# One encoder layer on one core: another order at the stage heads, second-half tokens and gate weights split ahead, half the norms moved

## The chip, the cores and the metric

The kernel runs on one core of one Trainium2 chip. The metric is the device time of one execution in microseconds (us). Before the change three executions took 2854.31, 2856.01 and 2858.43 us; the median is 2856.01.

## What is computed

The reference is one layer of a bidirectional encoder over 2048 tokens of width 1024, in float32:

```
u    = rmsnorm(x)
proj = u @ w_in                       # 1024 -> 2304: qa ka va qb kb vb
o_a  = rmsnorm(windowed attention, 8 heads, 2 key/value heads, window 128, sink, bias)
o_b  = rmsnorm(mixture of 3 dilated attentions, 8 heads, patterns (128,1) (512,4) (2048,16))
h    = x + rmsnorm(concat(o_a, o_b) @ w_o)
h    = h + rmsnorm(relu(rmsnorm(h) @ w_up)**2 @ w_down)      # 1024 -> 4096 -> 1024
h    = h + rmsnorm(sigmoid(h @ w_gate + b) * (p @ w_ple))    # p: 2048 x 256
```

## The kernel before

**Products.** Every float32 matrix is split into a high part, a rounded copy that ScalarE writes, and a low part, the rest, that VectorE subtracts (`split`, L125, and `split_scaled`, L129, which also multiplies by a gain). A product is three matmuls, high x high, high x low and low x high (L133 to L137, and L171 to L173 where the three are issued piece by piece).

**Engines and order.** SP issues the loads and most stores, ScalarE the stores of projections and of `pled`. The head and the last stage are ordered by the framework's scheduler. From attention A to the end of the MLP the order is written by hand: time is counted in ticks, `later(dt, fn)` puts a step dt ticks ahead, `tick()` runs what is due, and each engine executes its instructions in the order in which they were issued. A tile pool with a tag has a number of slots; a new tile waits until the last user of the slot is done. `raws` (tag wraw) has two slots, `sg` (tag sgt) two, `vr` (tag vraw) two.

**Head.** `prep_tile` (L248) loads a tile of 128 tokens, takes its mean square on ScalarE (`rms`, L120 to L123), the power on GpSimd (L117), scales it on GpSimd (L253), transposes it on TensorE (L144) and splits it (L126, L127). Four tiles make a block of 512 tokens. Four chunks of 128 columns of w_in are loaded and split in 8 pieces each (L130 on ScalarE, L131 on VectorE) before the first projection; then each block goes through the four chunks, and one tile of the next block is prepared after each of them.

**Attention A** has four pairs of heads with 16 items each. At item n = 3 of a pair the next pair's q (`a_half`, GpSimd copies of L233) and bias are fetched. The rest of the q and k projections fills TensorE between the items.

**Attention B** has four pairs of heads; for each the patterns p = 2, 0, 1, and for each pattern eight items. In the first items the kernel issues the loads of v and of biases (`load_text`, then GpSimd copies), of `sel`, and of the first four row blocks of W_o (`load_wo`, `load_wo_k`), which are split by ScalarE and VectorE two ticks after their load, one after the other. Products with the first half of W_o are the filler from tick 11 of the stage on, `ple()` (p @ w_ple) from tick 86. `ple` copies each result from PSUM with ScalarE into an `sgt` tile and stores it to `pled` (L912 to L918). After the last item the mixers of the last pair run out, with two pieces of filler a tick (L976).

**Stage C** (32 steps s, L1280) multiplies by the second half of W_o, adds the first, and does residual and norms. Tokens of the first half are transposed and split into the `vt` tiles; those of the second half go as float32 to `vsp` in DRAM (L1080, L1081). W_up's first chunks are loaded at s = 8 and 15 (`up_weights`, L1111).

**MLP.** Two halves of 1024 tokens; half n // 16, 16 rounds each, 28 ticks a round. Round n runs `down` of its own 256 columns of the hidden layer, as seven products of 2x2 blocks (28 pieces of three matmuls, L1205), and beside it `up` of the next round (L1187). VectorE adds the results to eight `acc` tiles (L1214) and GpSimd does the seventh part (L1212); GpSimd makes the sums and differences of blocks (`combo`, L1105), `pair_of` splits them (L1099, L1100). `up` of round 15 of a half (issued in round 14, and in round 30) is followed by `reload` (L1133): for i = 0, 1 the next content of `vt[i]`, the second half's tokens from `vsp` or the gate's weights, is loaded in four parts and split (L1136 ScalarE, L1137 VectorE, 128x1024 each). At the end of the first half `post` (L1215) does, for each of its eight tiles, squares on ScalarE (L1253), sum and power, the scale on VectorE (L1262), the add of h on GpSimd (L1265) and the store to `hd`; it reads and writes the `acc` tiles, which the second half's first products need again (L1208).

**Last stage.** 16 items of h @ w_gate with the weights in `vt`, from about 2650 us on.

Of the kernel before, what the change touches and what calls it, by code (L numbers as in the profile page):

```python
# [12 lines left out]
F32 = mybir.dt.float32  # L13
# [46 lines left out]
def layer(ctx, tc, a, out):  # L60
# [31 lines left out]
    vsp = dram.tile([2, 128, 8, 512], F32, name="vsp")  # L92
    pled = dram.tile([S, D], F32, name="pled")
# [147 lines left out]
    with ExitStack() as st:  # L241
        pst = st.enter_context(tc.tile_pool(name="pst", bufs=3, space=PSUM, reuse_waits="tile"))
        psm = st.enter_context(tc.tile_pool(name="psm", bufs=5, space=PSUM, reuse_waits="tile"))
        with ExitStack() as st1:
# [3 lines left out]
            def prep_tile(tb, j):  # L248
# [3 lines left out]
                r = rms(xt, xn)  # L252
# [179 lines left out]
    with ExitStack() as st:  # L432
# [38 lines left out]
        def a_item(pair, n):  # L471
# [92 lines left out]
        def feed(t):  # L564
            if t == 57:
# [3 lines left out]
                st_b["b"] = {(0, 2): load_b3(0)}  # L569
            next(fill, None)  # L570
# [53 lines left out]


# [4 lines left out]
    with ExitStack() as st:  # L630
# [11 lines left out]
        def load_bias(pair, i):  # L642
# [12 lines left out]
            def part(hh):  # L655
                text, b = load_text(i, 2 * pair + hh), bs[hh]
                later(2, lambda: copies(text, b))
# [14 lines left out]
        def load_sel():  # L672
            def part(hf):
                raw = raws.tile([32, S // 2], F32, name="sraw", tag="wraw")
                sp.dma_start(raw, a["sel"][:, hf * S // 2 : (hf + 1) * S // 2])
                later(2, lambda: act.activation(sel[:, hf * S // 2 : (hf + 1) * S // 2], raw, AF.Copy))
# [4 lines left out]
        def b_item(pair, p, bank, half):  # L681
# [197 lines left out]
        def ple():  # L879
# [26 lines left out]
            for t in range(16):  # L906
                ph_, pl_ = cur
                for hf in range(2):
# [6 lines left out]
                    mx = sg.tile([128, 512], F32, name="sgt", tag="sgt")  # L915
# [59 lines left out]
        pipe.drain()  # L975
        while mixers:  # L976
            advance()
            next(fill2, None)
            next(fill2, None)
# [131 lines left out]
    def up_weights():  # L1111
# [4 lines left out]
        hl = upw[g] = [fus[g % 3].tile([128, 8, 128], F32R, name="up" + n, tag="up" + n) for n in "hl"]  # L1116

        def hi(q):
# [320 lines left out]
```

## Time and profile before

| | |
|---|---|
| profiled execution, own time | 2857.3 us |
| its span | 2855.5 us |
| mean granted TensorE clock | 0.982 |
| TensorE, matmuls | 2732.8 us (96%) |
| VectorE | 1732.7 us (61%) |
| ScalarE | 1275.2 us (45%) |
| GpSimd | 943.1 us (33%) |
| DMA | 280.86 MB, mean 98 GB/s |

The profile is one execution, with times counted from the start of its span. Engines are called PE (TensorE), PEld (its weight loads), DVE (VectorE), ACT (ScalarE), POOL (GpSimd) and SP (the engine that issues most DMAs). The granted clock is a share of 2.4 GHz; 0.50 is the lower of its two levels, 1.2 GHz, and a mean between 0.50 and 1.00 is a mixture. Busy time says how much an engine does in a stretch; what it waited for is in the waits, and there each wait is put down to the instruction that ended it.

### The profile page before, as it was taken

To read this page: it belongs to the slowest core of one execution; us is meant where nothing else is said; L and a number is where in the kernel's file an instruction comes from. 1 tells how busy PE (TensorE), PEld (TensorE's weight loads), DVE (VectorE), ACT (ScalarE), POOL (GpSimd) and SP (SyncE) were. 2 spreads that over 40 slices of the span, in tenths; PEclk is the share of its full clock that TensorE was granted. 3 is DMA by queue.
4 is the path that set the end of the run, shared out by engine and by line. 5 is a ranking of instruction groups with operands and counts; after the bars stand their busy time and mean duration, and the time that the engine had idled before them with its cause. 6 is when DMAs were issued, how large, how long until landed. Compare 5 with 4: busy or idle time off the path is not lost.

```text
span 2855.5 us, 38726 instructions
## 1 busy us (share of the span) xinstructions
PE 2732.8 (96%) x13952; PEld 2140.4 (75%) x13952; DVE 1732.7 (61%) x3394; ACT 1275.2 (45%) x2928; POOL 943.1 (33%) x942
## 2 busy tenths in 40 slices
PE   7999999997999998999999999998999999998998
PEld 5778866665677776777888888886788888886787
DVE  3210234446656663676777777778777777777665
ACT  4321345556565653556344434445444344344322
POOL 2100033331322311435344334436443344344130
PEclk9999999998999999999999999998999999999999
DMA  5232352315424424772111111214211111112453
GB/s 167 80 122 78 100 159 65 108 65 153 128 72 122 96 93 153 256 249 89 45 59 45 45 59 45 67 63 155 93 45 45 59 45 59 45 52 96 159 195 104
DMA packets 230544, 280.86 MB, mean 98 GB/s; under 512 B 18320, under 2 KB 173968, under 8 KB 227952
## 3 DMA queue, kind: packets, MB, share of 16 engines
q1 hardware_dynamic: 203216, 238.21, 27.1%
q10 hardware_dynamic: 27136, 40.18, 3.9%
q8 instruction: 110, 1.80, 0.3%
q14 instruction: 82, 0.67, 0.1%
HBM read 204.62 MB, written 81.07 MB: 100 GB/s over the span
## 4 chain that ended last, share of the span: by engine, by line
PE 50%; DVE 3%; POOL 1%; issue 1%; ACT 0%; DMA 0%; POOLq 0%; DVEq 0%; SPq 0%; ACTq 0%
PE psd L1205 11%; PE psy L1205 9%; PE psu L172 8%; PE psu L173 8%; PE psu L171 8%; PE psm L135 2%; PE psm L136 2%; PE psm L137 2%; DVE acc L1214 1%; DVE vt L1137 1%; PE pst L144 0%; DVE al L1100 0%; POOL h L1265 0%; DVE dnl L1100 0%; DVE acc L1262 0%
## 5 line engine op out<-in xcount | busy, mean ns | idle before, releaser
L1214 DVE TENSOR_TENSOR acc<-acc,psd 128x512 f32<-128x512 f32 x488 | 332.0, 686 | 197.4 <-PE psd L1205 192.4
L172 PE MATMUL psu<-vt,uph 128*128 128x512 f32 x1024 | 408.8, 399 | 0.0
L173 PE MATMUL psu<-vt,upl 128*128 128x512 f32 x1024 | 406.3, 397 | 0.0
L171 PE MATMUL psu<-vt,uph 128*128 128x512 f32 x1024 | 403.6, 394 | 0.0
L1105 POOL TENSOR_TENSOR tmp<-rl 128x512 f32<-128x512 f32 x64 | 84.0, 1312 | 669.8 <-ACT rl L1193 669.8
L1214 DVE TENSOR_TENSOR acc<-acc,psy 128x512 f32<-128x512 f32 x248 | 170.3, 687 | 107.4 <-PE psy L1205 101.2
L172 PEld LDWEIGHTS psu<-vt,uph 128*128 128x128 f32 x1024 | 193.2, 189 | 48.3
L171 PEld LDWEIGHTS psu<-vt,uph 128*128 128x128 f32 x1024 | 193.7, 189 | 45.3
L745 ACT ACTIVATE e<-e,tm 128x256 f32<-128x256 f32 (+1 forms) x384 | 177.3, 463 | 109.1 <-DVE tm L742 106.9
L173 PEld LDWEIGHTS psu<-vt,upl 128*128 128x128 f32 x1024 | 193.0, 188 | 43.9
L1212 POOL TENSOR_TENSOR acc<-acc,dmp 128x512 f32<-128x512 f32 x128 | 194.3, 1529 | 52.1 <-DVE al L1100 31.5
L1205 PE MATMUL psd<-dnh,ah 128*128 128x512 f32 x512 | 202.6, 396 | 3.1 <-DVE acc L1214 3.1
L1192 ACT ACTIVATE rl<-psu 128x512 f32<-128x512 f32 x128 | 76.4, 597 | 288.8 <-PE psu L173 288.8
L1205 PE MATMUL psd<-dnh,al 128*128 128x512 f32 x512 | 203.9, 398 | 0.0
L131 DVE SCALAR_TENSOR_TENSOR wc<-wraw,pre_mix_t,wc 128x128 fp32r<-128x128 f32 x176 | 57.9, 375 | 239.8 <-ACT wc L130 239.8
L1205 PE MATMUL psd<-dnl,ah 128*128 128x512 f32 x512 | 202.2, 395 | 0.0
L171 PE MATMUL psm<-uhi,wc 128*128 128x512 f32 x448 | 182.0, 411 | 3.7 <-ACT uhi L126 3.7
L742 DVE CUSTOM_DVE_ANT_0 e<-ps_s,b 128x256 f32<-128x256 f32 (+1 forms) x384 | 122.8, 376 | 102.4 <-PE ps_s L729 102.4
L172 PE MATMUL psm<-ulo,wc 128*128 128x512 f32 x448 | 178.0, 398 | 0.0
L173 PE MATMUL psm<-uhi,wc 128*128 128x512 f32 x448 | 177.4, 396 | 0.0
L1205 PE MATMUL psy<-dnh,ah 128*128 128x512 f32 x384 | 154.3, 402 | 18.0 <-DVE acc L1214 10.2
L1205 PE MATMUL psy<-dnh,al 128*128 128x512 f32 x384 | 154.4, 402 | 3.8 <-DVE al L1100 3.8
(692 smaller groups left out, 6247.1 us busy)
## 6 DMA issues: line engine op xcount, KB each, us to landing
upraw<-in_w_up_dram SPq DMA_DIRECT2D x64, 512.0 KB, 4.4
dnraw<-in_w_down_dram SPq DMA_DIRECT2D x64, 512.0 KB, 5.0
xt<-in_x_dram SPq DMA_DIRECT2D x32, 512.0 KB, 4.9
h<-hd SPq DMA_DIRECT2D x32, 512.0 KB, 3.9
wraw<-in_w_in_dram SPq DMA_DIRECT2D x26, 512.0 KB, 4.5
qkd<-sgt ACTq DMA_DIRECT2D x52, 256.0 KB, 2.4
mad<-sgt ACTq DMA_DIRECT2D x32, 256.0 KB, 2.3
pled<-sgt ACTq DMA_DIRECT2D x32, 256.0 KB, 2.0
```

Source lines behind the costliest of these rows:

```text
L131: dve.scalar_tensor_tensor(lo, src, g, hi.bitcast(F32), op0=ALU.mult, op1=ALU.subtract)
L135: pe.matmul(ps, lh(k), rh(k), start=k == 0, stop=False)
L171: pe.matmul(ps, lh(k), rh(k), start=k == 0, stop=False)
L172: pe.matmul(ps, lh(k), rl(k), start=False, stop=False)
L173: pe.matmul(ps, ll(k), rh(k), start=False, stop=k == n - 1)
L742: dve.tensor_tensor_reduce(ej, box["ps"][hh][:, 256 * jj : 256 * jj + w], bs[hh] if p == 2 else bs[hh][:, var], scale=1.0, scalar=3.0e38, ...
L745: act.activation(ej, ej, AF.Exp, bias=tm, scale=-1.0, accum_out=box["dn"][p][:, i : i + 1])
L1105: pool.tensor_tensor(t, x, y, op=op)
L1192: act.activation(rl, ps, AF.Relu)
L1205: pe.matmul(ps, l[:, js], r, start=start and m == 0, stop=m == 2, skip_group_check=True)
L1212: pool.tensor_tensor(t, t, d, op=ALU.add)
L1214: dve.tensor_add(t, t, ps)
```

## The change

- Head: odd tiles of block 0 take their squares on VectorE; the first chunk's splits stand half after tile 2 and half after tile 3; the other three chunks are loaded and split inside block 0's loop, each before its own projection; the next block's tiles are prepared as (0, 1), (2), (3), ().
- Attention A: the first pair's prefetch is at item 6 instead of 3.
- Start of B: the two bias texts of pair 0 are loaded at tick 60 of A; the W_o row blocks are loaded at ticks 2, 2, 6, 7 and each is split four ticks after its load; other loads at 10, 12, 18; sel's copies four ticks after their load.
- End of B: from t = 4 on, ple's copies go to eight slots in one tile; the first three mixer loops take three pieces of filler.
- Stage C: a third `up_weights` at s = 28, split six ticks later.
- MLP: `split_job` loads one 128x512 block of the second half's tokens (rounds 1 to 14) or of the gate's weights (rounds 17 to 28), splits it and stores both parts to `spl`; `reload` only loads them. The first half's `acc` tiles are stored to `yd` at the end of round 15, and `post_job` does their norms, one tile a round, in rounds 17 to 24.

```diff
             prep_tile(0, 0)
             prep_tile(0, 1)
-            wk = load_chunk(w1, 512)
+            wk, raw = w1.tile([128, 2, 8, 128], F32R, name="wc", tag="wc"), load_raw(512)
             prep_tile(0, 2)
+            split_chunk(wk, raw, range(4))
             prep_tile(0, 3)
+            split_chunk(wk, raw, range(4, 8))
             first = [(wk, 512)]
-            for c, pl in ((VA0, w1), (0, wcp), (128, wcp)):
-                first.append((load_chunk(pl, c), c))
             for tb in range(4):
-                for n, (w, c) in enumerate(first):
-                    run(proj_chunk(w, c, tb, psm, pst, "pst"))
-                    if tb < 3:
-                        prep_tile(tb + 1, n)
+                for n in range(4):
+                    if tb == 0 and n < 3:
+                        c, pl = ((VA0, w1), (0, wcp), (128, wcp))[n]
+                        first.append((load_chunk(pl, c), c))
+                    run(proj_chunk(*first[n], tb, psm, pst, "pst"))
+                    for j in ((0, 1), (2,), (3,), ())[n]:
+                        if tb < 3:
+                            prep_tile(tb + 1, j)
...
-                if n == 3 and pair < 3:
+                if n == (3 if pair else 6) and pair < 3:
...
+    def load_wo_first(to):
+        def part(k):
+            halves = load_wo_k(*((wcp, "wc", 2) if k < 2 else (wop, f"wo{k}", 1)), k)
+            later(4, lambda: to.append(halves()))
+
+        for k, dt in enumerate((0, 0, 4, 5)):
+            later(dt, lambda k=k: part(k))
...
-                        st_b["b"][0, 0] = load_bias(0, 1)
-                        later(3, load_sel)
-                        later(5, lambda: load_wo(0, st_b["wa"]))
-                        later(6, lambda: st_b["b"].update({(0, 1): load_bias(0, 2)}))
-                        later(6, lambda: st_b["v"].update({(0, 1): load_v(0, 1)}))
+                        st_b["b"][0, 0] = load_bias(0, 1, st_b["text"])
+                        later(2, lambda: load_wo_first(st_b["wa"]))
+                        later(10, lambda: st_b["b"].update({(0, 1): load_bias(0, 2)}))
+                        later(12, lambda: st_b["v"].update({(0, 1): load_v(0, 1)}))
+                        later(18, load_sel)
...
-                    mx = sg.tile([128, 512], F32, name="sgt", tag="sgt")
+                    if 2 * t + hf == 8:
+                        big = bm.tile([128, 8, 512], F32, name="pst", tag="v1")
+                    mx = big[:, (2 * t + hf) % 8] if t >= 4 else sg.tile([128, 512], F32, name="sgt", tag="sgt")
...
     def reload(i, half):
...
+        vt[i] = new_vt(i)
         def load(q):
...
+            for j in range(2):
+                sp.dma_start(vt[i][j][:, 2 * q : 2 * q + 2].bitcast(F32), spl[half][i][:, j, 2 * q : 2 * q + 2])
         for q in range(4):
-            later((1, 2, 6, 9)[q], lambda q=q: load(q))
+            later(1 + q, lambda q=q: load(q))
+
+    def split_job(half, i, k, at):
...
+        for dt, fn in ((0, fetch), (6, high), (7, low), (9, store)):
+            later(at + dt, fn)
+
+    def post_job(t, at):
...
+        for dt, fn in ((0, fetch), (6, lambda: squares(0)), (7, lambda: squares(1)), (8, rstd), (10, lambda: scale(0)),
+                       (11, lambda: scale(1)), (12, lambda: add(0)), (13, lambda: add(1)), (14, keep)):
+            later(at + dt, fn)
...
-        if s in (8, 15):
-            up_weights()
+        if s in (8, 15, 28):
+            up_weights(6 if s == 28 else 3)
...
+            if 1 <= n < 15:
+                for at in ((0, 14) if n < 3 else (0,)):
+                    split_job(0, *jobs[0].pop(0), at)
+            if 17 <= n < 30:
+                if n < 25:
+                    post_job(n - 17, 0)
+                for at in ((16,) if n < 20 else (0, 14) if n >= 25 else (16,)):
+                    if jobs[1]:
+                        split_job(1, *jobs[1].pop(0), at)
             if n == 15:
-                for t in range(4):
-                    later(14 + 3 * t, lambda t=t: post(0, accs, t, vr, sg, later))
+                for t in range(8):
+                    later(20 + (t // 2 if t < 4 else t), lambda t=t, accs=accs: sp.dma_start(yd[128 * t : 128 * t + 128, :], accs[t]))
```

In `split_job` fetch, high, low and store are a load of 256 KB, a ScalarE copy of 128x512, a VectorE subtraction of 128x512 and a store of 512 KB. In `post_job` fetch loads y and h (two loads of 512 KB into the two slots of vraw), squares are two ScalarE operations of 128x512, rstd three GpSimd operations of one column, scale and add two VectorE operations of 128x512 each, and keep a store of 512 KB.

## Rows read from the trace of the kernel before

**Rows 1.** The page: busy time, share and instructions of TensorE.

```profile
PE 2732.8 (96%) x13952; PEld 2140.4 (75%) x13952; DVE 1732.7 (61%) x3394; ACT 1275.2 (45%) x2928; POOL 943.1 (33%) x942
```

**Rows 2.** Stretches: length, busy per engine (instructions), TensorE clock, DMA share, GB/s.

```profile
0.00:30.00 30.00, 13.28 (x49) 10.35 (x50) 17.70 (x47) 21.67 (x54) 10.51 (x18) 1.00 0.83 245
390.00:400.00 10.00, 5.08 (x29) 3.52 (x28) 1.12 (x5) 2.27 (x7) 3.15 (x4) 0.85 0.45 144
630.00:690.00 60.00, 43.72 (x347) 31.69 (x346) 35.81 (x152) 37.53 (x134) 9.45 (x13) 0.78 0.68 188
1080.00:1100.00 20.00, 11.77 (x41) 8.21 (x40) 8.82 (x16) 6.41 (x13) 1.46 (x2) 0.83 0.46 147
1135.00:1145.00 10.00, 5.44 (x17) 4.18 (x18) 0.43 (x1) 2.65 (x5) 0.00 (x0) 0.83 0.58 197
1279.00:1290.00 11.00, 5.69 (x22) 4.17 (x20) 6.58 (x5) 7.58 (x15) 4.72 (x7) 0.84 0.75 267
1840.00:1882.00 42.00, 42.00 (x182) 33.83 (x181) 30.36 (x42) 17.25 (x31) 17.62 (x12) 1.00 0.16 50
1940.00:2020.00 80.00, 62.89 (x232) 48.82 (x231) 65.56 (x72) 38.48 (x83) 52.23 (x33) 0.87 0.43 143
2605.00:2660.00 55.00, 43.35 (x168) 32.71 (x167) 46.00 (x64) 27.69 (x54) 13.20 (x8) 0.91 0.40 143
2645.00:2660.00 15.00, 11.12 (x48) 8.62 (x47) 9.18 (x19) 8.19 (x26) 0.00 (x0) 0.89 0.47 172
```

**Rows 3.** ScalarE groups of 0-40 us, and a wait of 0-30: total, times, longest.

```profile
L130 ACT ACTIVATE wc<-wraw,pre_mix_t 128x128 fp32r<-128x128 f32 x32 | 10.0, 397 | 0.8 <-DMA wraw<-in_w_in_dram 0.7
L122 ACT ACTIVATE xn<-xt 128x1024 f32<-128x1024 f32 x7 | 7.4, 1056 | 4.4 <-DMA xt<-in_x_dram 4.4
...
PE pst L144 <- POOL xn L253: 15.5, 4, 9.3
```

**Rows 4.** Waits of 390-400 us.

```profile
POOL q L233 <- DMA wraw<-qkd: 7.6, 1, 7.6
```

**Rows 5.** Waits of 630-690 us.

```profile
PE ps_s L729 <- DVE tm L742: 9.5, 3, 9.1
...
ACT wo L130 <- DMA wraw<-in_w_o_dram: 8.2, 1, 8.2
```

**Rows 6.** Waits of 1130-1147 us.

```profile
ACT sgt L916 <- DMA pled<-sgt: 6.3, 2, 4.9
```

**Rows 7.** Waits of 1270-1295 us.

```profile
ACT vs L1080 <- DMA vsp<-vs: 5.4, 2, 3.8
```

**Rows 8.** VectorE groups of 1925-2025 us: busy, mean ns, idle before.

```profile
L1262 DVE SCALAR_TENSOR_TENSOR acc<-acc,rstd,gb 128x1024 f32<-128x1024 f32 x8 | 14.2, 1781 | 3.7 <-POOL rstd L117 3.7
...
L1137 DVE TENSOR_TENSOR vt<-vraw,vt 128x1024 fp32r<-128x1024 f32 x5 | 10.1, 2030 | 0.0
```

**Rows 9.** VectorE in order of time, a steady round: start, us, [idle before].

```profile
1850.11 1.78 DVE L1100 TENSOR_TENSOR al<-tmp,ah 128x512 fp32r<-128x512 f32 x1
...
1854.23 0.68 DVE L1100 TENSOR_TENSOR dnl<-tmp,dnh 128x512 fp32r<-128x512 f32 x1
...
1856.42 0.69 DVE L1214 TENSOR_TENSOR acc<-acc,psd 128x512 f32<-128x512 f32 x1 [0.71 <-PE psd L1205]
...
1859.21 0.69 DVE L1214 TENSOR_TENSOR acc<-acc,psy 128x512 f32<-128x512 f32 x1 [0.62 <-PE psy L1205]
...
1861.30 0.69 DVE L1214 TENSOR_TENSOR acc<-acc,psy 128x512 f32<-128x512 f32 x1 [0.34 <-PE psy L1205]
```

**Rows 10.** GpSimd in order of time, the same round.

```profile
1854.27 1.80 POOL L1105 TENSOR_TENSOR tmp<-dnraw 128x512 f32<-128x512 f32 x1
```

**Rows 11.** SP's waits, 1700-1866 us.

```profile
SPq L1160 <- DVE dnl L1100: 78.2, 4, 19.7
```

**Rows 12.** VectorE groups of 2605-2660 us.

```profile
L1137 DVE TENSOR_TENSOR vt<-vraw,vt 128x1024 fp32r<-128x1024 f32 x8 | 11.8, 1489 | 1.0 <-ACT vt L1136 1.0
```

**Rows 13.** The page, DMA issues: count, size, median us from issue to landing.

```profile
h<-hd SPq DMA_DIRECT2D x32, 512.0 KB, 3.9
```

More of the change, by code (lines that the diff above doesn't have):

```diff
@@ L92, in layer @@
     vsp = dram.tile([2, 128, 8, 512], F32, name="vsp")
+    spl = [[dram.tile([128, 2, 8, 512], F32, name=f"spl{n}{i}") for i in range(2)] for n in "vg"]
+    yd = dram.tile([S // 2, D], F32, name="yd")
     pled = dram.tile([S, D], F32, name="pled")
@@ L569, in feed @@
                 st_b["b"] = {(0, 2): load_b3(0)}
+            if t == 60:
+                st_b["text"] = [load_text(1, hh) for hh in range(2)]
             next(fill, None)
@@ L640, in op_of, with load_bias @@
             return (1, 2, 0 if pair % 2 == 0 else 3)[p]
-        def load_bias(pair, i):
+        def load_bias(pair, i, texts=None):
             bs = []
@@ L655, in part @@
             def part(hh):
-                text, b = load_text(i, 2 * pair + hh), bs[hh]
-                later(2, lambda: copies(text, b))
+                text, b = texts[hh] if texts else load_text(i, 2 * pair + hh), bs[hh]
+                later(0 if texts else 2, lambda: copies(text, b))
             for hh in range(2):
@@ L675, in part @@
                 sp.dma_start(raw, a["sel"][:, hf * S // 2 : (hf + 1) * S // 2])
-                later(2, lambda: act.activation(sel[:, hf * S // 2 : (hf + 1) * S // 2], raw, AF.Copy))
+                later(4, lambda: act.activation(sel[:, hf * S // 2 : (hf + 1) * S // 2], raw, AF.Copy))
             part(0)
@@ L975, in layer @@
         pipe.drain()
+        loops = 0
         while mixers:
             advance()
-            next(fill2, None)
-            next(fill2, None)
+            for _ in range(3 if loops < 3 else 2):
+                next(fill2, None)
+            loops += 1
             tick()
@@ L1109, in layer, with up_weights @@
     upw, ups = {}, {"next": 0, "live": 0, "busy": 0}
-    def up_weights():
+    def up_weights(ahead=3):
         g = ups["next"]
@@ L1125, in up_weights @@
         for q in range(2):
-            later(3 + 2 * q, lambda q=q: hi(q))
-            later(4 + 2 * q, lambda q=q: lo(q))
+            later(ahead + 2 * q, lambda q=q: hi(q))
+            later(ahead + 1 + 2 * q, lambda q=q: lo(q))
     def feed_up():
@@ L1133, in reload @@
     def reload(i, half):
-        def part(q, raw):
-            k = 2 * q
-            act.activation(vt[i][0][:, k : k + 2], raw, AF.Copy)
-            later(1, lambda: dve.tensor_sub(vt[i][1][:, k : k + 2], raw, vt[i][0][:, k : k + 2].bitcast(F32)))
+        vt[i] = new_vt(i)
         def load(q):
-            raw = vr.tile([128, 2, 512], F32, name="vraw", tag="vraw")
-            src = w_g[:, 2 * q : 2 * q + 2, 512 * i : 512 * i + 512] if half else vsp[i, :, 2 * q : 2 * q + 2, :]
-            sp.dma_start(raw, src)
-            later(4 if q == 0 else 3, lambda: part(q, raw))
@@ L1145, in reload, with fetch, high, low @@
-        vt[i] = new_vt(i)
-        for q in range(4):
-            later((1, 2, 6, 9)[q], lambda q=q: load(q))
+            for j in range(2):
+                sp.dma_start(vt[i][j][:, 2 * q : 2 * q + 2].bitcast(F32), spl[half][i][:, j, 2 * q : 2 * q + 2])
+        for q in range(4):
+            later(1 + q, lambda q=q: load(q))
+    def split_job(half, i, k, at):
+        box = {}
+        def fetch():
+            box["raw"] = vr.tile([128, 512], F32, name="vraw", tag="vraw")
+            sp.dma_start(box["raw"], w_g[:, k, 512 * i : 512 * i + 512] if half else vsp[i, :, k])
+        def high():
+            box["hl"] = vr.tile([128, 2, 512], F32R, name="vhl", tag="vraw")
+            act.activation(box["hl"][:, 0], box["raw"], AF.Copy)
+        def low():
+            dve.tensor_sub(box["hl"][:, 1], box["raw"], box["hl"][:, 0].bitcast(F32))
+        def store():
+            sp.dma_start(spl[half][i][:, :, k], box["hl"].bitcast(F32))
+        for dt, fn in ((0, fetch), (6, high), (7, low), (9, store)):
+            later(at + dt, fn)
@@ L1310, in layer @@
         vr = mlp3.enter_context(tc.tile_pool(name="vr", bufs=2, reuse_waits="tile"))
-        accs = None
+        jobs = [[(i, k) for i in range(2) for k in range(8)] for _ in range(2)]
         for n in range(32):
```

44 lines of the change are left out of this document (38 added, 6 removed).

## The prediction

> **What bounds the kernel now.** I read the page first: TensorE is busy for 2732.8 of 2855.5 us [rows 1], so it sets the time nearly everywhere, and what an edit can win is TensorE idle time plus time at a lowered granted clock. Then I cut the span into stretches and looked for those where TensorE's busy time is short or its clock is below 1.00 [rows 2]. For each I take the loss as (length - busy) + (1 - clock) x busy. The reader is to see that the loss sits in eight places, and that each is one that the diff touches: 0-30: 16.7; 390-400: 4.9 + 0.8 = 5.7; 630-690: 16.3 + 9.6 = 25.9; 1080-1100: 8.2 + 2.0 = 10.2; 1135-1145: 4.6 + 0.9 = 5.5; 1279-1290: 5.3 + 0.9 = 6.2; 1940-2020: 17.1 + 8.2 = 25.3; 2605-2660: 11.65 + 3.9 = 15.5. Together 111 us. The steady round 1840-1882 has no loss: 42.0 us busy at 1.00, with VectorE at 30.4, ScalarE at 17.3 and GpSimd at 17.6 of 42. There TensorE is the bound and the others have slack, which is what the change spends. Last I read for each place the waits, for what ended them.
>
> **Part by part.** Every sum is made against the profiled execution, 2857.3 us (a span of 2855.5 and 1.8 around it); the median of the three runs, 2856.0, is 1.3 below that.
>
> *Head (L249-269).* Removed from ScalarE ahead of the first projection: two squares of 1.06 us (L122) and up to 24 of the 32 L130 pieces, 10.0 x 24/32 = 7.5 us [rows 3]. Added to VectorE: two reduces over 128x1024, whose nearest row is L1262, 1.78 us [rows 8]; VectorE is busy for 17.7 of these 30 us, so they lie beside other work. TensorE waits 15.5 us for xn [rows 3]; its longest wait, 9.3, is the arrival of the first tile and stays, 6.2 is the chain of the later tiles. Ends: 2 (the two squares alone) and 10 (squares and pieces together). I take 6, the row of 6.2, because the chain of the later tiles runs through exactly the engine that is relieved. The later weight pieces now stand beside the first block's matmuls; if they come late there, the lower end is what is left.
>
> *Prefetch of attention A (n = 6 instead of 3).* GpSimd waited 7.6 us for the q load [rows 4], TensorE stood for 4.9 us behind it, and the clock was 0.85 over those 10 us [rows 2]. Three items later the load is no longer queued behind the relay of v. Ends 0 (the same wait, later) and 5.7; I take 5.
>
> *Start of attention B (L564-760).* TensorE waits 9.1 us in one piece for VectorE's tm, and in the same stretch ScalarE waits 8.2 us for the transfer of a W_o row block [rows 5]. That load is now issued at tick 2 and used four ticks after issue, the bias texts are loaded before the stage, and filler matmuls start some nine ticks earlier. Gone: the 9.1 and the clock behind it.  Added wait: sel's copy at tick 22 shares the two slots of raws with the o and W_o loads; ScalarE stands in order behind it, and the exponentials behind that, 2 to 3 us if it is late. The filler matmuls aren't saved, only moved into idle time, so of the 25.9 at most the 16.3 idle can go. Ends 3 and 16; I take 9, the one wait.
>
> *End of B, ple (L916).* ScalarE waits 6.3 us in two pieces for pled stores that hold its two slots [rows 6]; with eight slots this goes: 5 of the 5.5 lost at 1135-1145. A third fill in the first three mixer loops puts a few matmuls into 1080-1100: 1.5 (0 to 4). Together 6.5, ends 3 and 9.5.
>
> *End of stage C (up_weights at s = 28).* TensorE loses 6.2 while ScalarE waits 5.4 for vsp slots [rows 7] with the queues full (1279-1290, 267 GB/s on average). One of the loads there (512 KB, 2 us at that rate) now goes ahead. Ends 0 and 5; I take 2.5.
>
> *Boundary of the MLP's halves (rounds 14 to 18 before).* Removed from it: VectorE's splits (five of 128x1024 in 1925-2025, 10.1 us), the eight scales (14.2 us) [rows 8], and what GpSimd and ScalarE do for them. With VectorE at 65.6 of 80 us in 1940-2020 [rows 2] this is what fills it. Added: 4.2 MB of yd stores and 2 x 4.2 MB of loads of split tokens. Half a round, 21 us, has to carry each load of 4.2 MB: 16 us at the 267 GB/s of 1279-1290 [rows 2]. It fits, with little left for the yd stores beside it. Ends 10 and 25.3; I take 20, all but 5, for weights and stores that now meet on one queue.
>
> *End of the MLP.* The gate's eight splits, 11.8 us of VectorE [rows 12], leave the last rounds. Of the 15.5 lost, 5.1 lies in 2645-2660 (3.9 idle, 0.11 x 11.1 = 1.2 clock) [rows 2], where the norms of the last tiles stand: it stays. So 10.4 can go; ends 5 and 10.4; I take 9.
>
> *What the rounds now carry.* Thirty-two split jobs, one VectorE and one ScalarE operation each, spread one or two to a round: VectorE has 11.6 us idle in a round. Cost 0 to 6 over all, I take 1. Eight post jobs, one a round in rounds 17 to 24: two squares on ScalarE, three small GpSimd operations, and four VectorE operations over 128x512 in ticks 10 to 13 (a tick is 42/28 = 1.5 us). In those ticks of a steady round VectorE idles 0.71, 0.62 and 0.34 = 1.7 us [rows 9]. Behind the queued operations are the L1214 adds that free psy, and TensorE waits for those; each add has about 1.5 us to spare (two ticks from the end of a piece to the next use of its bank, 3.0, less the piece's three matmuls at 42.0/182 = 0.23 and the add's 0.69). One post operation costs between 0.68 (L1100 in its light form) and 1.78 (the same line while GpSimd works) [rows 9]. Four are 2.7 to 7.1 us; less 1.7 idle and 1.5 spare, TensorE stands 0 to 3.9 us a round, 0 to 31 in eight. L1262's 1.78 for 128x1024 makes 0.89 for a half, and 4 x 0.89 = 3.6 gives 0.4 a round: I take 3.
>
> Sum: 6 + 5 + 9 + 6.5 + 2.5 + 20 + 9 - 1 - 3 = 54. 2857.3 - 54 = 2803.3; on the median's footing 2802.
>
> **Rivals.**
>
> *VectorE backs up behind the post jobs.* For it: GpSimd has most of its work in the first half of a round, so the heavy price of 1.78 may be the usual one. Against it: L1100 at 1854.23 took 0.68 [rows 9] while GpSimd began an operation of its own, which then took 1.80 [rows 10]. The Trainium skill, "SBUF — State Buffer", section "SBUF: two separate sides", says that a VectorE operation with two SBUF inputs and a GpSimd operation reading SBUF hold one port pair by an exclusive lock: who starts first has it, the other waits it out. Both rows agree with that; by it the four operations cost the heavy end wherever GpSimd starts first and the light end wherever VectorE does.
>
> All four operations at 1.78 in all eight rounds: 31 instead of 3, so 2830.
>
> *Transfers bind the boundary.* Between the middle of round 14 and the end of round 15, 63 us, 12.6 MB (two loads, the yd stores) and some 2 MB of weights have to pass: 232 GB/s, against 245 at 0-30 and 267 at 1279-1290. The yd stores wait on SP's in-order queue for the last adds of round 15, with the next round's weights behind them. For it: the rates are close to each other. Against it: the rates of the rows are averages with idle queues in them. Then half of 20 and a third of 9 are lost: 2802 + 13 = 2815.
>
> *The early edits don't do what they say.* Head, prefetch, B, ple and C bring their low ends, 2 + 0 + 3 + 3 + 0 = 8 instead of 29, because the next wait stands right behind each: 2823. For it: in 630-690 several waits end last one after the other. Against it: in 390-400 and 1135-1145 there is one only.
>
> *Slower than before: SP's queue delays the fetches of the jobs.* SP stands up to 19.7 us in one wait for a free slot of dnraw [rows 11]. A fetch queued behind such a wait lands after tick 6; then ScalarE waits for it in order, its relu and dmp copies behind it, and TensorE after 1.5 us to spare. A fetch 5 us late costs 5 - 1.5 = 3.5 a round; 26 rounds carry jobs (1 to 14 and 17 to 28), 91 us in place of the 4 for jobs in the sum: 2889. It decides from 58/26 = 2.2 us a round. Against it: the slot waits end about when the program reaches the load's own tick, so a fetch issued at tick 0 should go out on time, six ticks (9 us) ahead of its use, and the loads of h, of the same size, land in 3.9 [rows 13].
>
> **How the numbers follow.** Forecast, with its own range of 2785 to 2818: 0.55. VectorE's backlog 0.12, transfers 0.15, early edits 0.11, slower 0.07. The good ends together, 10 + 5.7 + 16 + 9.5 + 5 + 25.3 + 10.4 = 82, give 2774; the range runs from 2775 to 2836, which takes in the first three rivals and leaves out the last and mixtures of the others. About 0.2% (5.7 us) is what a measurement of this kernel can tell from no change. Slower by more than that: the last rival, 0.07, and 0.01 for two others together; within it: 0.03 from mixtures; faster 0.89.
>
> **What would show it.** Right: TensorE without a gap of over 2 us at 1940-2020 and 2605-2645, no ScalarE wait for pled, first projection some 6 us earlier, W_o matmuls from the start of B, clock at 1.00 there. In rounds 17 to 24, rounds of 42 to 42.5 us; 45 would be the backlog. ScalarE waiting for vraw or y1 in many rounds would be the slower case; TensorE waiting for vt or upl after the boundary, the transfers. The forecast is wrong above all if the boundary keeps more than 10 of its 25 us, or the post rounds lose over 2 us each.

## The result: 2816.2 us, 1.4% faster, and 14 us short of the forecast

Four executions of the changed kernel took 2813.91 to 2817.90 us, median 2816.24; the kernel before, beside it, 2855.45. The ratio is 0.9861 with a 95% interval of 0.9843 to 0.9878. The forecast was 2802 (2775 to 2836): the sign and the range hold, the gain is 39 us where 54 were forecast. The profiled execution is the quickest of the four (2813.91, a span of 2812.1), so the stages below add up to 43.4 where the medians differ by 39.2.

TensorE's row on the page after answers to [rows 1]:

```profile
PE 2719.5 (97%) x13952; PEld 2123.9 (76%) x13952; DVE 1767.2 (63%) x3420; ACT 1273.4 (45%) x2940; POOL 931.5 (33%) x950
```

The stretches after that answer to [rows 2] (length; busy on PE, PEld, DVE, ACT, POOL with instructions; TensorE clock; DMA share; GB/s). Everything stands earlier by what was gained before it.

```profile
0.00:30.00 30.00, 15.15 (x55) 11.16 (x56) 19.34 (x48) 19.08 (x49) 11.74 (x18) 0.83 0.82 239
617.00:677.00 60.00, 51.83 (x430) 37.54 (x428) 42.99 (x181) 42.17 (x157) 13.45 (x20) 0.91 0.65 186
1047.00:1071.00 24.00, 16.60 (x79) 11.50 (x77) 8.18 (x16) 10.63 (x23) 0.00 (x0) 0.93 0.47 149
1096.00:1121.00 25.00, 22.44 (x102) 17.05 (x101) 6.22 (x14) 10.82 (x21) 5.24 (x8) 1.00 0.71 219
1236.00:1262.00 26.00, 20.48 (x100) 16.18 (x99) 20.26 (x18) 16.28 (x30) 11.28 (x15) 0.93 0.76 246
1890.00:1932.00 42.00, 42.00 (x183) 33.80 (x182) 30.50 (x44) 17.15 (x30) 17.76 (x12) 1.00 0.60 225
1932.00:1974.00 42.00, 42.00 (x182) 33.83 (x181) 23.58 (x27) 25.57 (x46) 18.52 (x12) 1.00 0.37 126
1976.00:2020.00 44.00, 42.33 (x180) 33.33 (x179) 35.76 (x47) 18.71 (x36) 18.53 (x16) 1.00 0.27 86
2577.00:2608.00 31.00, 25.23 (x102) 18.92 (x100) 25.33 (x37) 8.65 (x16) 12.24 (x8) 0.94 0.52 204
```

The start of B lost 16.3 us of TensorE in its first 60 and now loses 8.2. At the boundary of the MLP's halves (1890 to 1974) TensorE is busy without a gap at full clock, where 17.1 idle us stood at 1940-2020. But 1976-2020, a round with a post job, has 1.7 idle, and no such round had any before; and in the last round of the MLP (2577-2608) 5.8 us of idle are left.

The timeline gives the same by stages, from one fixed instruction to the next (first score of A, first and last score of B, first product of stage C, first and last product of `down`, end; inside the MLP the first of a round's four relus, the copies that ScalarE makes of `up`'s results, and the last one of all). The stages follow one another, so the differences add up to the change of the span, 43.4 us:

| stage | before | after | gained | forecast |
|---|---|---|---|---|
| head, to A's first score | 366.3 | 360.0 | 6.4 | 6 |
| attention A | 263.9 | 257.3 | 6.6 | 5 |
| B, first to last score | 429.1 | 414.2 | 14.9 | 9 |
| mixers and ple, to stage C | 90.8 | 89.1 | 1.7 | 6.5 |
| stage C | 144.7 | 141.4 | 3.3 | 2.5 |
| MLP, boundary (relus of round 15 to 18) | 152.1 | 125.7 | 26.4 | 20 |
| MLP, eight post rounds (relus of round 18 to 26) | 335.1 | 354.5 | -19.3 | -3 |
| MLP, last relu to last down | 31.7 | 27.6 | 4.1 | 9 |
| the other rounds (split jobs) | | | 0.0 | -1 |
| last stage | 203.7 | 204.4 | -0.7 | 0 |

Six places gave what was forecast or more. Three did not: the post rounds, the end of the MLP, and ple.

### The profile page after: what moved, and what is told of

The parts are those of the page before. It is cut to its first block, busy times and chain, and to the rows that moved or that the text cites. A ratio compares the mean times of both kernels' runs of the same rounds, so it can differ in the third digit from the quotient of the medians.

```text
span 2812.1 us, 38924 instructions
## 1 busy us (share of the span) xinstructions
PE 2719.5 (97%) x13952; PEld 2123.9 (76%) x13952; DVE 1767.2 (63%) x3420; ACT 1273.4 (45%) x2940; POOL 931.5 (33%) x950
## 4 chain that ended last, share of the span: by engine, by line
PE 54%; DVE 4%; issue 2%; POOL 1%; ACT 1%; DMA 1%; ACTq 0%; DVEq 0%; POOLq 0%; SPq 0%
PE psd L1288 11%; PE psy L1288 9%; PE psu L174 8%; PE psu L175 8%; PE psu L173 8%; PE psm L137 3%; PE psm L138 3%; PE psm L139 3%; DVE y L1219 1%; PE psd L137 1%; PE psd L139 1%; PE psd L138 1%; DVE acc L1297 1%; POOL acc L1295 1%; DVE y L1223 1%
## 5 line engine op out<-in xcount | busy, mean ns | idle before, releaser
L1297 DVE TENSOR_TENSOR acc<-acc,psd 128x512 f32<-128x512 f32 x488 | 331.3, 685 | 179.5 <-PE psd L1288 174.6
L1297 DVE TENSOR_TENSOR acc<-acc,psy 128x512 f32<-128x512 f32 x248 | 168.8, 684 | 79.2 <-PE psy L1288 72.5
```

The source lines that it names most:

```text
L1297: dve.tensor_add(t, t, ps)
```

## The experiments

Stage lengths below are those of the table, from one profile each. Stages that a kernel doesn't touch vary between kernels: B with the new order 414.2 to 419.7, stage C 141.4 to 144.6, mixers and ple 88.0 to 90.7, attention A 257.3 to 258.3, while the MLP's steady rounds all take 41.9. (The last section says why, for B.) So verdicts rest on the stage that was edited. The whole times of e3, e7, u2 and u6 came out 1 to 3.5 us above every range of times that was named for them. Where an edit undoes a part of the change, its minus lines are the changed kernel's. e2 and e7 leave work out and are there for their timing alone.

**e1_post_late.** The theory of the lost 19 us: VectorE's four post operations, beside GpSimd.

```diff
-                    post_job(n - 17, 0)
-                for at in ((16,) if n < 20 else (0, 14) if n >= 25 else (16,)):
+                    post_job(n - 17, 11)
+                for at in ((0, 14) if n >= 25 else (0,)):
```

> Same work, but in rounds 17 to 24 the gate's split job stands at tick 0 and the post job at tick 11, so that its scales and adds are issued in ticks 21 to 24 when GpSimd is idle. Theory (VectorE's backlog in ticks 10 to 13, four operations at 0.68 to 1.78 us beside GpSimd, behind them the adds that free psy): the eight rounds of 44.3 us fall to 41.9 to 42.2, the four operations take 0.68 to 0.70 each, the time is 2797 (2794 to 2801). Rival (the post job's squares on ScalarE, its DMAs or its place on SP's queue cost the 2.4 us): they are all still there, rounds stay at 43.5 to 44.3 and the time at 2811 to 2816.

Measured: 2800.66 us (0.9813 of before, 0.9796 to 0.9829). All eight rounds take 41.9, and 335.1 us stand again between the relus of rounds 18 and 26. The theory holds; the time lies in the range, 3.7 above the point that was named. In the profiles B, ple and C, which the edit doesn't touch, are 6.7 us longer here than in the changed kernel, but this profile is the slowest of its four executions and that one the quickest of its four.

VectorE's groups of 1975-2330 us in the changed kernel (busy, mean ns, idle before):

```profile
L1219 DVE SCALAR_TENSOR_TENSOR y<-y,rstd,gb 128x512 f32<-128x512 f32 x16 | 23.7, 1481 | 1.6 <-POOL rstd L1215 1.6
...
L1223 DVE TENSOR_TENSOR y<-y,h 128x512 f32<-128x512 f32 x16 | 17.1, 1068 | 0.0
```

And of 1960-2300 us with the late post jobs (seven of the eight):

```profile
L1185 DVE TENSOR_TENSOR vhl<-vraw,vhl 128x512 fp32r<-128x512 f32 x8 | 14.3, 1783 | 0.0
L1219 DVE SCALAR_TENSOR_TENSOR y<-y,rstd,gb 128x512 f32<-128x512 f32 x14 | 10.4, 745 | 0.0
L1223 DVE TENSOR_TENSOR y<-y,h 128x512 f32<-128x512 f32 x14 | 9.5, 681 | 0.0
```

The same operations fall from 1481 to 745 ns and from 1068 to 681 (0.68 to 0.70 us had been named for all). The split job's subtraction, which now stands at tick 7, pays the heavy price in their place (1783 ns, 684 at tick 23), and nobody waits for it: the adds behind it in ticks 8 to 11 free banks that TensorE needs again only at tick 20.

**e2_post_no_dve.** Is it VectorE at all, or the squares, the DMAs, SP's queue?

```diff
-        for dt, fn in (..., (8, rstd), (10, lambda: scale(0)), (11, lambda: scale(1)), (12, lambda: add(0)), (13, lambda: add(1)), (14, keep)):
+        for dt, fn in (..., (8, rstd), (14, keep)):
```

> The post jobs stay at tick 0 but leave out their four VectorE operations (the scale and the add of h for the first half's tokens). Theory (VectorE's queue): rounds 17 to 24 at 41.9, time about 2797. Rival (squares, loads, stores and the three GpSimd operations, which all remain): rounds at 43 or more, time 2806 to 2816.

Measured: 2796.97 us, the eight rounds 335.1 us together. Squares, loads, stores and the three GpSimd operations are all there and cost nothing.

**e7_scales_only.** How much can such a round absorb?

```diff
-        ... (11, lambda: scale(1)), (12, lambda: add(0)), (13, lambda: add(1)), (14, keep)):
+        ... (11, lambda: scale(1)), (14, keep)):
```

> The post jobs stay at tick 0 and leave out the two adds of h (ticks 12 and 13), the two scales in ticks 10 and 11 stay. Theory (a round loses what the operations take beyond the 1.7 us that VectorE idles there and about 1.5 us that the adds of psy have to spare): 2 x 1.48 + 0.2 for the rstd stays under 3.2, so rounds 17 to 24 take 41.9 to 42.3, time 2797 to 2802. Rival (no spare: every us of VectorE there shows): half the loss stays, rounds of 43.0 to 43.5, time 2806 to 2811.

Measured: rounds of 43.4 us (347.1 for the eight), 2813.45 us. The expectation fell on the rival's side: half of the operations keep 1.5 of the 2.4 us (the time is above both ranges). TensorE's wait in 1980-2330 us of this kernel (total, times, longest):

```profile
PE psy L1288 <- DVE acc L1297: 8.8, 7, 1.3
```

The order on VectorE in a post round of the changed kernel, and TensorE's longest wait in it, show what was left out of the sum (start, us):

```profile
1990.54 1.78 DVE L1219 SCALAR_TENSOR_TENSOR y<-y,rstd,gb 128x512 f32<-128x512 f32 x1 [0.20 <-POOL rstd L1215]
...
1992.85 1.18 DVE L1219 SCALAR_TENSOR_TENSOR y<-y,rstd,gb 128x512 f32<-128x512 f32 x1
1993.95 1.78 DVE L1127 TENSOR_TENSOR al<-tmp,ah 128x512 fp32r<-128x512 f32 x1
1995.65 0.67 DVE L1297 TENSOR_TENSOR acc<-acc,psy 128x512 f32<-128x512 f32 x1
1996.25 1.47 DVE L1223 TENSOR_TENSOR y<-y,h 128x512 f32<-128x512 f32 x1
...
1998.24 0.68 DVE L1223 TENSOR_TENSOR y<-y,h 128x512 f32<-128x512 f32 x1
```

```profile
1996.47 0.47 PE L1288 MATMUL psy<-dnh,ah 128*128 128x512 f32 x1 [1.27 <-DVE acc L1297]
```

The al split in the same place of the steady round before:

```profile
1857.02 0.97 DVE L1100 TENSOR_TENSOR al<-tmp,ah 128x512 fp32r<-128x512 f32 x1
```

The add for which TensorE waits is the one at 1995.65. Ahead of it stand 1.78 + 1.18, the 0.20 wait for rstd, and the al split, which took 0.97 before and takes 1.78 now: 0.81 more, 4.0 us together. Of the 1.7 us of idle that the forecast set against it only the 0.71 ahead of tick 10 lies before that add [rows 9]; the other two lie behind. 4.0 - 0.71 - 1.3 of stall leaves about 2.0 that the add could spare (1.5 had been estimated). By the same sum two scales at 0.75, the 0.20 and al's 0.81, 2.5 us together, would have left no wait at this add even in the old place. That is an estimate: e1 changes the price and the place of the operations together, and no run tries one without the other.

**u6_post_boundary.** What did moving the norms buy at the boundary?

```diff
-                accs = [acc_tile(t) for t in range(8)]
+                old, accs = accs, [acc_tile(t) for t in range(8)]
+                if old:
+                    for t in range(4, 8):
+                        later(3 * (t - 4), lambda t=t: post(0, old, t, vr, sg, later))
...
-                    post_job(n - 17, 0)
...
-                for t in range(8):
-                    later(20 + (t // 2 if t < 4 else t), lambda t=t, accs=accs: sp.dma_start(yd[128 * t : 128 * t + 128, :], accs[t]))
+                for t in range(4):
+                    later(14 + 3 * t, lambda t=t: post(0, accs, t, vr, sg, later))
```

> Undoes one part: the first half's norms stand at the boundary again, as post with its scale over 128x1024 on VectorE and its add on GpSimd; no yd, no post jobs; the second half's tokens are still split ahead and loaded by DMA. Theory (splits and norms together filled VectorE there, and the acc tiles are free only after the norms): from the relus of round 15 to those of round 18 133 to 145 us, against 152.1 before and 125.7 after the change; rounds 17 to 24 at 41.9; time 2804 to 2816. Rival (the splits alone had filled it): 125.7 to 129, time 2797 to 2800, and moving the norms wasn't needed.

Measured: 145.9 us from the relus of round 15 to those of round 18 (0.9 above what was named; 152.1 before, 125.7 after the change), post rounds back at 335.1, 2819.31 us (2804 to 2816 had been named). So splitting ahead alone is worth 6.2 of the 26.4, and moving the norms as well 20.2 more; no run moves the norms without the splits. In the changed kernel 19.3 of these 20.2 were paid again in the post rounds. VectorE's scale and ScalarE's wait for the `acc` tiles in this kernel (groups of 1930-1990, waits of 1880-1990):

```profile
L1345 DVE SCALAR_TENSOR_TENSOR acc<-acc,rstd,gb 128x1024 f32<-128x1024 f32 x7 | 13.0, 1854 | 3.7 <-POOL rstd L119 3.7
```

```profile
ACT acc L1291 <- POOL h L1348: 10.9, 3, 6.0
```

**e3_end_dve.** The end of the MLP kept 4.2 + 1.4 us idle.

```diff
-            elif n == 1:
+            elif n == 1 and not last:
...
-            d = down(fc, *work, accs)
+            d = down(fc, *work, accs, n == 31)
```

> In round 31 alone the seventh part is added by VectorE straight from PSUM (four operations of 0.69) in place of a ScalarE copy and a GpSimd add each (four of 1.72 in a row). Theory (the end kept 4.2 + 1.4 us of TensorE idle because GpSimd's four adds stand ahead of the sum that ScalarE's ah needs): both gaps go, rounds end 3 to 5 us earlier, last down matmul 53 to 55 us after the last relu of round 30 instead of 57.8, time 2811 to 2813. Rival (VectorE is the bound of that round whoever adds: 25 us of its operations against 26 us of the round): the gap goes but VectorE is 2.8 us longer, and the time stays at 2815 to 2817.

Measured: 25.7 us from the last relu to the last down product instead of 27.6, so a gain of 1.9 in its own stage, between the theory's 3 to 5 and the rival's nothing. (The expectation counts from the first of the last four relus, which it calls the last of round 30: 55.9 for 57.8.) The time, 2818.03 us (0.9872, 0.9856 to 0.9888), doesn't show it: in its profile B alone came out 5.4 us longer. The largest gap falls to 2.1, but VectorE now works without a pause from 2589.3 to 2605.4, as the rival has it.

**e4_late_and_sum.** Is it the order on GpSimd's queue?

```diff
-        at(36, lambda: set_(s, 4, lambda: combo(x[1, 0], s[2], ALU.subtract)))
+        at(31 if last else 36, lambda: set_(s, 4, lambda: combo(x[1, 0], s[2], ALU.subtract)))
...
-                prepare((n + 1) % 16, x, xs, ws)
+                prepare((n + 1) % 16, x, xs, ws, last=n == 30)
```

> The late post jobs of the first experiment, and in round 31 the last sum of blocks that GpSimd makes (s4) is issued ahead of its four adds instead of behind them. Theory (the 4.2 us of TensorE idle in the last round were ScalarE's ah behind that sum, behind four adds of 1.72): the gap falls under 1.5 us, from the last relu of round 30 to the last down matmul 53.5 to 55 us instead of 57.7, time 2796 to 2798 with the post rounds at 41.9. Rival (VectorE's 33 operations and GpSimd's adds set that round, whatever the order): 57 us or more, time 2800 as in the first experiment.

Measured: 2797.12 us (0.9792, 0.9778 to 0.9805), post rounds at 41.9, but 28.0 us from the last relu to the last down product where e1 has 27.5: none gained. The theory fell, although the time lies in its range: the MLP is 0.5 us longer than e1's, so the 3.5 us under e1's time aren't the edit's. TensorE's waits in the last round, first in the changed kernel (2565-2620), then here (2560-2600):

```profile
PE psy L1288 <- DVE acc L1297: 4.2, 1, 4.2
...
PE psy L1288 <- ACT dmp L1294: 1.4, 1, 1.4
```

```profile
PE psy L1288 <- DVE acc L1297: 3.9, 1, 3.9
```

The sum is early now, and yet VectorE is late, for another reason. ScalarE's and VectorE's order of time in this kernel:

```profile
2572.85 0.60 ACT L1294 ACTIVATE dmp<-psy 128x512 f32<-128x512 f32 x1 [1.98 <-POOL acc L1295]
2574.56 0.60 ACT L1294 ACTIVATE dmp<-psy 128x512 f32<-128x512 f32 x1 [1.11 <-POOL acc L1295]
2575.05 0.62 ACT L1126 ACTIVATE dnh<-tmp 128x512 fp32r<-128x512 f32 x1
```

```profile
2575.71 1.83 DVE L1127 TENSOR_TENSOR dnl<-tmp,dnh 128x512 fp32r<-128x512 f32 x1 [1.15 <-ACT dnh L1126]
```

ScalarE's copy waits for a GpSimd add to free one of two sgt slots, its next split stands behind that copy, VectorE behind the split, the adds behind VectorE. In this round TensorE has no `up` beside its pieces and comes through twice as fast (0.7 us a piece instead of 1.5), so the three engines barely keep up with it, and taking one wait away leaves the next.

**e5_late_end_dve.** The late post jobs and e3's adds together (both diffs above).

> The late post jobs and VectorE's own adds in round 31 together. Theory (the two losses lie in different rounds and add up): rounds 17 to 24 at 41.9, the last round 25.7 us from the last relu to the last down matmul (27.6 without the adds), time 1.9 us under the first experiment's, 2797 to 2800. Rival (in that round ScalarE, GpSimd and VectorE wait for each other, and another placing of the adds shifts the wait only): 27 us or more, time as in the first experiment, 2800 to 2802.

Measured: 2797.18 us (0.9793, 0.9779 to 0.9806); post rounds 335.1; the last part 25.7. The MLP takes 1324.6 us, the least of all kernels (before 1357.0, changed 1345.8, e1 1326.4). The two gains add up. In time it stands level with e4, which has the MLP 2.3 us longer and stage C 1.2 shorter. Its own gain repeats e3's 25.7; 27 or more, the rival's, is excluded.

**u3_b_order.**

```diff
-                        later(2, lambda: load_wo_first(st_b["wa"]))
-                        later(10, lambda: st_b["b"].update({(0, 1): load_bias(0, 2)}))
-                        later(12, lambda: st_b["v"].update({(0, 1): load_v(0, 1)}))
-                        later(18, load_sel)
+                        later(3, load_sel)
+                        later(5, lambda: load_wo(0, st_b["wa"]))
+                        later(6, lambda: st_b["b"].update({(0, 1): load_bias(0, 2)}))
+                        later(6, lambda: st_b["v"].update({(0, 1): load_v(0, 1)}))
```

> Undoes one part: at the start of attention B the loads of sel, W_o, biases and v stand at the old ticks 3, 5, 6, 6 and W_o's blocks are split one after the other (sel's copies and the early texts stay new). Theory (the W_o wait of 8 to 9 us and the late filler were what was lost there): from the first to the last score of B 422 to 430 us, against 414 to 420 in the four kernels with the new order; time 2824 to 2832. Rival (the early texts or the later prefetch in A brought most of it): 416 to 420, time 2816 to 2820.

Measured: B 426.8 us, 2829.25 us. The old order of these four loads costs 7 to 13 us (against 419.7 to 414.2). Its waits of 617-677 us answer to [rows 5]:

```profile
PE ps_s L752 <- DVE tm L765: 13.4, 4, 6.7
ACT wo L132 <- DMA wraw<-in_w_o_dram: 9.5, 2, 8.9
```

The theory holds for the W_o wait and not for "the late filler". The first product with W_o, the filler, stands behind the same 136 scores in the kernel before, in the changed kernel and here: the order never moved it. What changed is how long TensorE needs to get there. B cut at that product, before, after and here (length; busy; clock; DMA share; GB/s):

```profile
630.24:695.42 65.18, 48.37 (x388) 35.55 (x387) 40.84 (x171) 42.59 (x152) 10.40 (x15) 0.80 0.62 174
695.42:1059.30 363.88, 350.50 (x2719) 265.17 (x2719) 236.88 (x888) 216.92 (x750) 95.05 (x135) 0.97 0.39 104
```

```profile
617.23:671.96 54.73, 46.56 (x388) 33.41 (x387) 40.67 (x171) 40.39 (x150) 10.99 (x15) 0.91 0.69 195
671.96:1031.38 359.42, 346.04 (x2719) 261.52 (x2719) 236.47 (x888) 218.10 (x752) 94.95 (x135) 0.98 0.39 106
```

```profile
618.96:686.71 67.75, 49.09 (x387) 35.67 (x387) 40.37 (x171) 42.60 (x152) 10.88 (x15) 0.82 0.59 161
686.71:1045.75 359.04, 345.64 (x2719) 261.08 (x2719) 236.62 (x888) 216.34 (x750) 95.00 (x135) 0.98 0.39 106
```

So 10.5 of B's 14.9 us were gained ahead of the first filler (16.8 us of idle became 8.2, the clock rose from 0.80 to 0.91), and the old order gives all of it back. The other 4.5 lie behind it, with the same idle time (13.38) and a higher clock. The old order keeps them (359.0), and the kernels with the new one have 359.4 to 364.9 there, a spread that takes in the 363.9 before, so they aren't the edit's. Which of the four loads matters was not tried by itself.

**u2_prefetch3.**

```diff
-                if n == (3 if pair else 6) and pair < 3:
+                if n == 3 and pair < 3:
```

> Undoes one part: the first pair's prefetch in attention A is at item 3 again. Theory (GpSimd's q copy waits for its load behind the relay of v, and TensorE behind it): a TensorE gap of 4 to 5 us near 390 and a clock under 0.9 behind it, the stretch from the first score of A to the first of B 262 to 264 us instead of 257 to 258, time 2820 to 2822. Rival (the gap had come from the head's timing, which is new): under 1.5 us, 257 to 259.

Measured: attention A 262.8 us against 257.3, 2823.21 us; the waits of 384-396 us are those of [rows 4] again, with TensorE 4.7 us behind them (4.9 in that stretch before):

```profile
POOL q L235 <- DMA wraw<-qkd: 7.4, 1, 7.4
...
PE pt L526 <- POOL e L481: 4.7, 1, 4.7
```

**u4_head_squares.**

```diff
-                if tb == 0 and j % 2 == 1:
-                    ...
-                else:
-                    r = rms(xt, xn)
+                r = rms(xt, xn)
```

> Undoes one part: the squares of block 0's odd tiles go back to ScalarE; the order of chunks, splits and preparations stays new. Theory (ScalarE relief and order share the 6.4 us of the head): first projection 1.5 to 3 us later than 22.6, first score of A at 361.5 to 363. Rival (the order of the chunks does all of it): first projection within 0.5 us of 22.6 to 23.4, first score of A at 359.5 to 361.

Measured: the first projection at 25.4 us, 2.0 to 2.8 later than in the others (22.6 to 23.4), A's first score at 361.7 (360.0 in the changed kernel, but 359.4 to 361.9 in the others, so at that point the squares can't be told from nothing), 2819.95 us. The squares on VectorE bring the first projection forward by their 2 to 3 us. The rest of the 6.4 is left for the order of chunks and tiles, by subtraction, and not tried by itself.

**u1_ple_two_slots.**

```diff
-                    if 2 * t + hf == 8:
-                        big = bm.tile([128, 8, 512], F32, name="pst", tag="v1")
-                    mx = big[:, (2 * t + hf) % 8] if t >= 4 else sg.tile([128, 512], F32, name="sgt", tag="sgt")
+                    mx = sg.tile([128, 512], F32, name="sgt", tag="sgt")
```

> Undoes one part: all of ple's copies go through the two sgt slots again, three fills in the first three mixer loops stay. Theory (the eight slots took the wait of 6.3 us for pled away): ScalarE waits 4 to 6.5 us for pled after 1095 us again, the stretch from the last attention-B score to the first stage-C product grows by 4 to 6 us, time 2820 to 2822. Rival (the third fill or the earlier W_o filler already took it): grows by under 1.5 us, 2816 to 2818.

Measured: mixers and ple 92.2 us, 2818.96 us. That is 1.5 to 4.2 above the kernels with eight slots (88.0 to 90.7): between the two expectations. The wait is back in its old size (waits of 1085-1124 us; compare [rows 6]), in six pieces of up to 2.0 where it had been two:

```profile
ACT sgt L939 <- DMA pled<-sgt: 7.9, 6, 2.0
```

So the eight slots are worth about 3 us, not 5. The kernel before had only 90.8 with that wait, 1.4 less than this one, which differs from it here by the third fill alone; that is within the spread of 2.7 between kernels, so whether the third fill costs something stays open. With eight slots TensorE's weight loads wait 3.0 us for GpSimd's o (L980), and ScalarE's wait for `pled` isn't quite gone, for the copies of the first four token tiles still take the two slots. From the last score to stage C, before and after:

```profile
ACT sgt L916 <- DMA pled<-sgt: 8.4, 3, 4.9
```

```profile
ACT sgt L941 <- DMA pled<-sgt: 2.5, 2, 2.1
```

**u5_no_third_up.**

```diff
-        if s in (8, 15, 28):
-            up_weights(6 if s == 28 else 3)
+        if s in (8, 15):
+            up_weights()
```

> Undoes one part: no third load of W_up at s = 28. Theory (the load that went ahead is worth about 2 us): from the first product of stage C to the first down matmul 144.5 to 146 us, against 141.4 to 144.6 (mean 143) in the nine kernels that have it. Rival (VectorE's norm behind GpSimd's rstd ends that wait in any case): 142 to 144.

Measured: stage C 144.9 us, 2820.40 us. That is 1.8 above the mean of the others and 0.3 above the highest: it leans to the theory and doesn't settle it. Waits of 1236-1262 us in the changed kernel answer to [rows 7]:

```profile
DVE acc L1094 <- POOL rstd L1050: 5.6, 3, 2.5
PE pst L1100 <- DVE acc L1094: 5.1, 2, 4.1
...
ACT vs L1107 <- DMA vsp<-vs: 3.9, 2, 2.8
```

ScalarE's wait for the vsp slots fell from 5.4 to 3.9; TensorE's 4.1 us gap there is now the norm behind GpSimd's rstd.

## Why the prediction was right, and where it was off

*Sign and range* came from reading idle TensorE time by place and what ended each wait. For the prefetch and the start of B the undoing runs brought the same waits back (7.4 for 7.6 us in A, 13.4 in four pieces for 9.5 in three in B), and the loads were the cause (u2, u3). That the total came as near as it did is in part luck: by stages, the post rounds, ple and the MLP's end fell short by 26.0 together, the others came out 15.4 above, and 4.5 of these are B's clock. By the prediction's own signs it was half wrong: the boundary kept none of its 25 us, but the post rounds lost 2.4 us each, and over 2 was to tell against it.

*What the rounds now carry: mis-sized, 3 for 19.3.* The mechanism was named, as a rival with 0.12: adds that free psy, queued behind post operations on VectorE (e1, e2). The forecast took 0.89 for a scale, half of L1262's 1.78, and 3.6 for all four. They took 1.48, 1.48, 1.07 and 1.07 = 5.1, and an al split beside them grew from 0.97 to 1.78: 5.9 us, and 0.2 for rstd. The rows for that price stood in front of the reader: 1.78 and 0.68 for one operation [rows 9]. The choice of a middle value was the error, for in ticks 10 to 13 GpSimd was running, and its own operations give the four their heavy price (the last section has the rule). Against GpSimd at rest (e1) it is 0.75 and 0.68. The spare time was set too low (1.5, about 2.0 measured) and the idle time too high, for two of its three pieces lie behind the add that TensorE waits for (e7). Of the rival's 31 us, 19 came.

*Boundary: 26.4 for 20, undersized,* and 1.1 above the upper end of 25.3. Five us had been kept back for transfers that meet on one queue, and a rival had them bind. Neither came: the stretch moved 225 GB/s at 1890-1932 with TensorE busy for all of it. Which of the two moves did it was not in the forecast: 20.2 of it are the norms, 6.2 the splits (u6).

*End of the MLP: 4.1 for 9.* The step that failed is "10.4 can go": the gate's splits left, and the wait behind them was not looked for. By the order of time it is a chain of ScalarE's copies, GpSimd's adds and VectorE's adds in a round without `up` (e4); taking the copies and GpSimd's adds out of it gives 1.9 back (e3, e5), and what holds the rest was not taken apart.

*End of B: 1.7 for 6.5.* The step that failed is that a wait's length is a gain. Most of the wait went (8.4 to 2.5), but only some 3 us hung on it (u1), and next to nothing was gained in the mixers' gap: 7.4 us of idle stand at 1047-1071 where 8.2 stood at 1080-1100, and ScalarE's wr waits 4.0 us there for VectorE's wt in both kernels.

*Start of B: 14.9 for 9*, of which 10.5 are the edit's and 4.5 the clock's (u3). The wait of 9.1 was the right one to count; the step that failed is "filler matmuls start some nine ticks earlier". Their place is the same in both kernels, from tick 11 on; the sign "W_o matmuls from the start of B" didn't come, and the clock there is 0.91, not 1.00. *Head, A and C* are within 2 us, but the head's sign was off: the first projection came 3.1 us earlier (25.7 to 22.6) where some 6 had been named, and with the squares undone it stood at 25.4 (u4), so the weight pieces taken out ahead of it gave next to nothing at that point.

*The slower rival* (fetches late behind SP's queue) did not occur: in post rounds no ScalarE wait for y, and rounds 1 to 14 took 41.9 with split jobs in them.

## What to carry to other kernels

An operation moved into a steady round costs nothing only where two things hold: the engine's idle time lies ahead of the instruction that the bounding engine waits for, and the operation's price is taken for what the other engines do in those ticks. Read both from the order of time of one round, tick by tick; the round's mean busy share (30 of 42) says neither. And when a large stall is removed, look for the next wait in the same place before writing down its whole length.

## What the runs showed of the hardware

*The price of a two-input VectorE operation* over 128x512 in SBUF was 0.68 to 0.75 us beside an idle GpSimd (one took 0.79, in e3), and from 0.68 up to 1.86 beside a working one in most kernels. In the kernel before and in u6, where GpSimd adds over 128x1024 (2.87 us at 1994.55 before), it reached 2.9. L1297, with one input in PSUM, stayed at 0.67 to 0.75. The heavy price isn't a second level but the rest of the neighbour's time. GpSimd in the post round shown above:

```profile
1990.47 1.30 POOL L1132 TENSOR_TENSOR tmp<-dnraw 128x512 f32<-128x512 f32 x1
1991.85 1.63 POOL L1132 TENSOR_TENSOR tmp<-dnraw,tmp 128x512 f32<-128x512 f32 x1
1993.44 1.74 POOL L1132 TENSOR_TENSOR tmp<-dnraw 128x512 f32<-128x512 f32 x1
1995.88 1.29 POOL L1132 TENSOR_TENSOR tmp<-dnraw,tmp 128x512 f32<-128x512 f32 x1 [0.69 <-DVE al L1127]
```

These end at 1991.77, 1993.48, 1995.18 and 1997.17; VectorE's operations that began beside them end at 1992.32, 1994.03, 1995.73 and 1997.72, each 0.55 us later. In the changed kernel's trace 264 such operations begin while a GpSimd operation of over 1 us runs: 230 take more than 0.8 us, and nine in ten of those end 0.547 to 0.554 us behind it. So the price of one can be read from GpSimd's order of time.

*The same instructions under another clock.* B's stretches differ between kernels that issue the same instructions there, although TensorE's idle time is the same to 0.01 us (13.38 and 13.37 us from the first product with W_o to the last score, in the changed kernel and in e7, which take 359.4 and 363.8 for it; all of B 414.2 and 419.7). What differs is the granted clock behind the gaps. The same place in the changed kernel and in e1 (length; busy; clock; DMA share; GB/s):

```profile
835.00:840.00 5.00, 3.13 (x19) 2.22 (x18) 4.37 (x16) 2.74 (x10) 0.00 (x0) 0.91 1.10 209
840.00:845.00 5.00, 5.00 (x30) 3.40 (x29) 1.76 (x12) 1.49 (x8) 1.96 (x3) 0.75 0.02 7
```

```profile
840.00:845.00 5.00, 3.58 (x10) 2.59 (x11) 2.99 (x14) 2.60 (x10) 1.36 (x2) 0.72 0.90 169
845.00:850.00 5.00, 5.00 (x27) 3.36 (x26) 1.73 (x11) 2.13 (x9) 0.60 (x2) 0.59 0.00 2
```

Behind the same three gaps of 0.9 to 1.0 us the clock is at its lower level for part of the time, here longer than there. Such places in attention and stage C would account for the 2811 to 2821 us between executions of e3; that is argued, for only one of these was profiled. In the MLP's rounds without a gap every kernel takes 41.9.
